# A fused matmul and rotary embedding on one core: half of the stores move to another issuing engine, two more block pairs, and GpSimd takes a slice of the multiply

## The chip, the core and the metric

The kernel runs on one core of a Trainium2 chip. That core has five engines, each with its own instruction stream: TensorE (PE in the profile), VectorE (DVE), ScalarE (ACT), GpSimd (POOL) and SyncE (SP). They wait for one another by semaphores that the kernel sets itself. DMAs are issued by SP and ACT here, each with a queue of its own (SP's is q1 in the profile, ACT's is q10: the bytes of their issues add up to the bytes of these queues); 16 DMA engines serve both queues.

The metric is the time of one execution on the device in microseconds (us). Three runs of the kernel before gave 150.59, 151.72 and 154.15 us, a median of 151.72 us. The execution that the profiler recorded took 151.62 us; its span, from the first to the last instruction, is 149.8 us.

## The reference

`x` is (16, 512, 768), the weight is 768 x 768, and there are 12 heads of 64 columns. The output is x times the weight, followed by a rotation inside each head:

```python
y = np.matmul(x, weight).reshape(batch, seq, n_heads, head_dim)
y1, y2 = y[..., :32], y[..., 32:]
out1 = y1 * cos1 - y2 * sin1
out2 = y2 * cos2 + y1 * sin2
out = np.concatenate([out1, out2], axis=-1)      # float32
```

`cos` and `sin` depend on the position in the sequence and on the column in the head, not on the batch or the head.

## The kernel before

**Tiles and groups.** The 8192 rows of x are 64 tiles of 128 rows, and four tiles are one group, so there are 16 groups (0 to 15; `LAST` is 15). The four tiles of a group have the same sequence positions and so the same cosines and sines. A group's product has 128 x 3072 values and fills six PSUM banks, ps0 to ps5, once; the next group fills the same banks again. The other two banks (pt0, pt1) hold transposed inputs.

**Two ways to transpose.** The matmul needs x with its hidden dimension on the partitions. A *single* tile is loaded whole by SP (`xs`, a ring of 11 buffers), cast to fp16 by ACT (`xc`), transposed by six PE instructions into PSUM (L232) and copied out by ACT (`xt`). A *block pair* is two tiles at once: it is loaded in four quarters of 192 KB (`xb`, a ring of 4 buffers, L201), whose rows in DRAM are cut into runs of 768 bytes, cast by ACT in one instruction (`xd`, 2 buffers) and transposed by VectorE in 32 x 32 blocks (`xp`, L252), with no work for PE. The set `BLOCKS` (L135) says which pairs (group, half) are block pairs: the second half of groups 3 to 14, and the first half of groups 5, 7, 9, 11 and 13, which makes 17 pairs. Of a block pair's quarters SP issues the first two and ACT the other two.

**Rotation.** A group's product is taken in three units of 1024 columns, u0, u1 and u2 (`units`, L259), which are banks ps0-1, ps2-3 and ps4-5. For each, VectorE multiplies the unit in PSUM by the cosines and by the sines in one instruction with 2048 results (L309), into a `tq` buffer (a ring of 5: three of their own and two in the memory of the raw weights, which the profile calls w_raw). GpSimd adds the two halves, one of them with its 32-column halves swapped, into the output buffer `ov` (L320). There are 4 `ov` buffers, one per group, so group g waits for the stores of group g - 4. Groups 14 and 15 go by smaller units, and the last three additions are VectorE's.

**Order.** One Python loop (L510) writes all instruction streams. Iteration i emits the matmuls of tile i; the rotation of a unit when its last column is done (u0 in the second tile of a group, u1 in the third, u2 in the fourth); the block transposes of pairs up to 6 tiles ahead (`bturns`); the PE transposes up to 3 tiles ahead (`turns`); and the casts up to 7 tiles ahead (`casts`). After each cast `pump` lets SP issue the loads that now have a free buffer, in the order of a sorted list; ACT's quarters come out of `casts` too. At the end of the iteration stands the group's store, if there is one: half a group (768 KB) at a time, two groups after its own, in `STORES`. Up to group 12 ACT issues all stores, later ones SP. Each engine works through its stream in order: what ACT has to wait for or is held up by delays everything that stands behind it on ACT.

The helper `Flow.do` (L42) records who wrote and read each buffer and puts the semaphore waits in front of an instruction.

Of the kernel before, what the change touches and what calls it, by code (L numbers as in the profile page):

```python
# [10 lines left out]
FP32 = mybir.dt.float32  # L11
FP16 = mybir.dt.float16
MULT = mybir.AluOpType.mult
ADD = mybir.AluOpType.add


class Flow:
# [24 lines left out]
    def do(self, e, make, reads=(), writes=(), dma=None, tick=True):  # L42
        need = {}
        for k in reads:
            for s, v in self.wrote.get(k, {}).items():
                need[s] = max(need.get(s, 0), v)
        for k in writes:
            for d in (self.wrote, self.readby):
                for s, v in d.get(k, {}).items():
                    need[s] = max(need.get(s, 0), v)  # L50
        if e == "pe":
            need.pop("pe", None)
        waits = self.settle(e, need)
        for s, v in waits[:-1]:
            self.eng[e].wait_ge(self.sem(s), v)  # L55
        i = make(self.eng[e])
        if waits:
            s, v = waits[-1]
            i.wait_op(self.sem(s), v, "sem-ge")
        name, step = (dma, 16) if dma else (e, 1)  # L60
        self.sem(name)
        at = self.count[name] + step
        if tick or dma:
            i.then_inc(self.sems[name], step)
            self.count[name] = at
            self.known[name, at] = dict(self.seen[e])
        for k in reads:
            d = self.readby.setdefault(k, {})
            d[name] = max(d.get(name, 0), at)
        for k in writes:  # L70
            self.wrote[k] = {name: at}
            self.readby[k] = {}
        return i
# [30 lines left out]
def kernel(  # L104
# [11 lines left out]
    f = Flow(nc, tc)  # L116
    do = f.do
    P = nc.NUM_PARTITIONS

    B, S, H = x.shape  # L120
    NH = int(n_heads)
    D = H // NH
# [9 lines left out]
    LAST = NG - 1  # L132


    BLOCKS = {(g, 1) for g in range(3, 15)} | {(g, 0) for g in (5, 7, 9, 11, 13)}  # L135

    def sbuf(name, shape, dt):
        return nc.alloc_sbuf_tensor(name, shape, dt).ap()

    NX, NB, NC, NCP, NXT, NXP, NTQ, NOV = 11, 4, 5, 2, 8, 4, 3, 4  # L140

    ident = sbuf("ident", [P, P], FP16)
    cold = sbuf("cold", [P, 512], FP16)
    sin_sb = sbuf("sin_sb", [P, SB, D], FP32)
    csn = sbuf("csn", [P, 2, SB, D], FP32)
# [8 lines left out]
    tq_b = [sbuf(f"tq{i}", [P, 2, 1024], FP32) for i in range(NTQ)]  # L154
    w_flat = w_raw.rearrange("p t e n -> p (t e n)")
    tq_b += [w_flat[:, ts(i, 2048)].rearrange("p (j n) -> p j n", j=2) for i in range(2)]
    W_HOME = [f"wr{t}{h}" for t, h in CHUNKS]
    ov_b = [sbuf(f"ov{i}", [P, QB * H], FP32) for i in range(NOV)]
    py = nc.alloc_psum_tensor("py", [P, 6 * 512], FP32).ap()
# [2 lines left out]
    def ring(name, n, state={}):  # L162
        k = state.get((id(f), name), 0)
        state[id(f), name] = k + 1
        return k % n

    def copy(e, o, i_):
        return lambda eng: (
            eng.copy(out=o, in_=i_) if e == "act" else eng.tensor_copy(out=o, in_=i_)  # L169
        )  # L170

    def where(i):
        g, s = divmod(i, QB)
        return QB * (g // SB) + s, g % SB

    def pair_of(i):
        return i // QB, (i % QB) // 2

    def is_block(i):
        return pair_of(i) in BLOCKS  # L180

# [55 lines left out]
    def cast_pair(gh, e="act"):  # L237
        k = xs[gh]
        c = ring("xd", NCP)
        xc[gh] = c  # L240
        do(e, copy(e, xd_b[c].rearrange("p (t j e) -> p t j e", t=NT, e=2),
                   xb_b[k].rearrange("p (j t e) -> p t j e", t=NT, e=2)),
           reads=[f"xb{k}q{q}" for q in range(NQ)], writes=[f"xd{c}"])
# [50 lines left out]

    ov_of = {}

    late = []

    def rope(g, u):
        c0, c1, ps, banks, adder = u  # L300
        w, r = c1 - c0, g % SB
        nh = w // D
        if adder == "dve":
            k = len(late)
            tq, keys = xs_b[k][:, 0 : 2 * w].rearrange("p (j n) -> p j n", j=2), [f"xs{k}"]
        else:
            k = ring("tq", NTQ + 2)
            tq, keys = tq_b[k][:, :, 0:w], [f"tq{k}"] + (W_HOME if k >= NTQ else [])
        do("dve", lambda eng: eng.tensor_tensor(  # L309
            out=tq.rearrange("p j (h d) -> p j h d", d=D),  # L310
            in0=ps.rearrange("p (h d) -> p h d", d=D)
            .unsqueeze(1).broadcast_to((P, 2, nh, D)),
            in1=csn[:, :, r, :].unsqueeze(2).broadcast_to((P, 2, nh, D)),
            op=MULT), reads=banks + ["csn"], writes=keys)
        if g not in ov_of:
            ov_of[g] = ring("ov", NOV)
        o = ov_of[g]

        def add():
            do(adder, lambda eng: eng.tensor_tensor(  # L320
                out=ov_b[o][:, ds(c0, w)].rearrange("p (h t d) -> p h t d", t=2, d=HD),
                in0=tq[:, 0].rearrange("p (h t d) -> p h t d", t=2, d=HD),
                in1=tq[:, 1].rearrange("p (h t d) -> p h t d", t=2, d=HD)[:, :, ::-1, :],
                op=ADD), reads=keys[:1], writes=[f"ov{o}c{c}" for c in range(c0, c1, 64)])

        if adder == "dve":
            late.append(add)
        else:
            add()

    def store(g, c0, c1, e):

        o = ov_of[g]
        b, r = where(g * QB)
        s0, s1 = c0 // H, -(-c1 // H)
        dst = out.rearrange("b (p r) h -> r p b h", r=SB)[r, :, b + s0 : b + s1]
        src = ov_b[o].rearrange("p (b h) -> p b h", b=QB)[:, s0:s1]
        if (c1 - c0) % H:
            dst = dst[:, 0, c0 - s0 * H : c1 - s0 * H]
            src = src[:, 0, c0 - s0 * H : c1 - s0 * H]  # L340
        do(e, lambda eng: eng.dma_start(out=dst, in_=src),
           reads=[f"ov{o}c{c}" for c in range(c0, c1, 64)], dma=f"ov{o}_{c0}")
# [5 lines left out]
        out=ident, in_=ident, compare_op=mybir.AluOpType.not_equal, fill=1.0,  # L348
# [3 lines left out]
    for k in order:  # L352
# [5 lines left out]
        out=csn[:, 0], in_=cos.rearrange("(p r) d -> p r d", r=SB)), writes=["cos"], dma="cos")  # L358
    do("sp", lambda eng: eng.dma_start(
        out=sin_sb, in_=sin.rearrange("(p r) d -> p r d", r=SB)), writes=["sin"], dma="sin")  # L360


    want = [(i, i) for i in range(QB, NTILE) if not is_block(i)]
    for g, h in BLOCKS:
        want += [(g * QB + 2 * h - 2.5 + 3 * q, ((g, h), q)) for q in (0, 1)]
# [41 lines left out]
    def castx(i, e):  # L407
        cast(i, e)
        xs_used[0] += 1
# [22 lines left out]
    for c in CHUNKS[3:5]:  # L432
# [5 lines left out]
        out=csn[:, 1, :, 0:HD], in_=sin_sb[:, :, HD:D]), reads=["sin"], writes=["csn1"])  # L438
    do("dve", lambda eng: eng.tensor_scalar_mul(
        out=csn[:, 1, :, HD:D], in0=sin_sb[:, :, 0:HD], scalar1=-1.0),  # L440
        reads=["sin", "csn1", "cos"], writes=["csn"])
    pump()

    state = {"cast": 4, "turn": 4, "bturn": 0, "half": 0}
    pairs = sorted(BLOCKS)

    def casts(upto):
        while state["cast"] < min(upto, NTILE):
            i = state["cast"]
            state["cast"] += 1  # L450
            if not is_block(i):
                castx(i, "act")
            elif i % 2 == 0:
                cast_pair(pair_of(i))
                xb_used[0] += 1
            pump()
            if state["half"] < 2 * len(pairs):
                n, q = divmod(state["half"], 2)
                g, h = pairs[n]
                if n < xb_used[0] + NB and i >= g * QB + 2 * h - LEAD:  # L460
                    load_quarter(pairs[n], 2 + q, "act")
                    state["half"] += 1
# [47 lines left out]
    for i in range(QB, NTILE):  # L510
        g, s = divmod(i, QB)
        us = units(g)
        done_to = (s + 1) * H
        for p in pieces(g, s):
            a, z, _, bank = p
            for c in CHUNKS:
                mm_piece(i, p, c, c == CHUNKS[0], c == CHUNKS[-1],
                         tick=c == CHUNKS[-1])
            for u in us:
                if u[1] == z:  # L520
                    rope(g, u)
        bturns(i + (B_AHEAD if i >= SETTLED else 3))
        turns(i + 1 + (T_AHEAD if i > QB + 1 else 2))
        casts(i + 1 + (C_AHEAD if i >= SETTLED else 3 if i == QB else 4))
        if i in STORES:
            o, k = STORES[i]
            store(o, 2 * H * k, 2 * H * (k + 1), "sp" if o > LAST - 3 else "act")
        if g == LAST:
            if s == 2:
                store(g, 0, H, "sp")  # L530
            if s == 3:
                store(g, H, 2 * H, "act")
# [3 lines left out]
    for k, add in enumerate(late):  # L536
        c = 3 * H + 256 * k
# [38 lines left out]
```

## Time and profile before

| | |
|---|---|
| median of three runs | 151.72 us |
| profiled execution, its span | 151.62 us, 149.8 us |
| busy share PE, DVE, POOL, ACT | 94%, 86%, 75%, 50% |
| mean DMA rate over the span | 355 GB/s |
| DMA rate in 45 to 110 us | 385 to 395 GB/s |
| granted TensorE clock | 0.99 |

An engine's busy share is an average over stages with different limits. What bounds a stretch is read from the chain of waits (which instruction followed which without a gap) and from the gaps in front of single instructions. A DMA's time to landing counts from its issue to its last completion signal.

### The profile page before, as it was taken

To read this page: it belongs to the slowest core of one execution; us is meant where nothing else is said; L and a number is where in the kernel's file an instruction comes from. 1 tells how busy PE (TensorE), PEld (TensorE's weight loads), DVE (VectorE), ACT (ScalarE), POOL (GpSimd) and SP (SyncE) were. 2 spreads that over 40 slices of the span, in tenths; PEclk is the share of its full clock that TensorE was granted. 3 is DMA by queue.
4 is the path that set the end of the run, shared out by engine and by line. 5 is a ranking of instruction groups with operands and counts; after the bars stand their busy time and mean duration, and the time that the engine had idled before them with its cause. 6 is when DMAs were issued, how large, how long until landed. Compare 5 with 4: busy or idle time off the path is not lost.

```text
span 149.8 us, 2471 instructions
## 1 busy us (share of the span) xinstructions
PE 141.2 (94%) x972; PEld 87.7 (59%) x972; DVE 128.7 (86%) x88; ACT 74.9 (50%) x76; POOL 112.8 (75%) x60
## 2 busy tenths in 40 slices
PE   6969999999999999999999999999999999999950
PEld 2435666666676655555666667565565666676730
DVE  0154999677999999999989999899989999998890
ACT  3444768886963280843563545444696118342100
POOL 1000299966897789887989889878988698999970
PEclk9999999999999999999999999999999999999995
DMA  4999999999999999999999999999999999997574
GB/s 129 346 400 399 404 348 293 287 297 260 227 323 399 390 373 384 388 386 387 389 382 396 391 395 396 398 385 395 399 410 410 418 413 417 396 403 311 229 278 152
DMA packets 33147, 53.11 MB, mean 355 GB/s; under 512 B 2288, under 2 KB 20464, under 8 KB 33136
## 3 DMA queue, kind: packets, MB, share of 16 engines
q10 hardware_dynamic: 16752, 27.79, 50.5%
q1 hardware_dynamic: 16384, 25.17, 48.7%
q8 instruction: 7, 0.11, 0.3%
q14 instruction: 4, 0.03, 0.1%
HBM read 27.79 MB, written 25.17 MB: 353 GB/s over the span
## 4 chain that ended last, share of the span: by engine, by line
PE 86%; DMA 5%; DVE 3%; SPq 1%; ACT 1%; issue 1%; ACTq 0%; DVEq 0%
PE py L291 80%; PE pt L232 6%; DMA w_raw<-in_weight_dram 5%; DVE xs L309 1%; ACT xc L169 1%; SPq L189 1%; DVE ov L320 1%; SPq L208 1%; DVE w_raw L309 0%; DVE w_sb L169 0%; ACTq L201 0%; DVE tq L309 0%; ACT xt L169 0%; DVEq L55 0%; SPq L571 0%
## 5 line engine op out<-in xcount | busy, mean ns | idle before, releaser
L320 POOL TENSOR_TENSOR ov<-tq 128x1024 f32<-128x1024 f32 (+2 forms) x33 | 69.0, 2107 | 27.4 <-DVE tq L309 25.7
L291 PE MATMUL py<-w_sb,xp 128*128 128x512 f16 (+1 forms) x408 | 69.4, 326 | 0.0
L309 DVE TENSOR_TENSOR tq<-py,csn 128x2048 f32<-128x2048 f32 (+2 forms) x33 | 65.8, 2015 | 3.8 <-PE py L291 3.5
L291 PE MATMUL py<-w_sb,xt 128*128 128x256 f16 (+1 forms) x360 | 60.8, 323 | 1.4 <-DVE w_sb L169 1.3
L291 PEld LDWEIGHTS py<-w_sb,xp 128*128 128x128 f16 x408 | 39.3, 98 | 24.6
L291 PEld LDWEIGHTS py<-w_sb,xt 128*128 128x128 f16 x360 | 34.2, 98 | 22.8 <-DVE w_sb L169 2.8
L320 POOL TENSOR_TENSOR ov<-w_raw 128x1024 f32<-128x1024 f32 (+2 forms) x21 | 43.6, 2087 | 4.2 <-DVE w_raw L309 4.2
L309 DVE TENSOR_TENSOR w_raw<-py,csn 128x2048 f32<-128x2048 f32 (+2 forms) x21 | 41.9, 1997 | 2.4 <-PE py L291 1.9
L169 ACT COPY xt<-pt 128x768 f16<-128x768 f16 x28 | 22.3, 800 | 31.9 <-PE pt L232 21.7
L169 ACT CAST xc<-xs 128x768 f16<-128x768 f32 x30 | 26.2, 905 | 17.7 <-issue 10.2
L169 ACT CAST xd<-xb 128x1536 f16<-128x1536 f32 x17 | 27.6, 1625 | 13.8 <-issue 5.0
L252 DVE STREAM_TRANSPOSE xp<-xd 128x768 f32<-128x768 f32 x17 | 16.4, 964 | 0.9 <-ACT xd L169 0.9
L232 PE MATMUL pt<-ident,xc 128*128 128x128 f16 x180 | 15.3, 222 | 0.2 <-ACT xc L169 0.2
L232 PEld LDWEIGHTS pt<-ident,xc 128*128 128x128 f16 x180 | 12.5, 99 | 5.2 <-ACT xc L169 1.8
L394 PE MATMUL py<-cold 128*128 128x512 f16 x12 | 5.3, 614 | 1.4 <-DVE cold L345 1.4
L169 DVE CAST w_sb<-w_raw 128x768 f16<-128x768 f32 x6 | 3.4, 558 | 3.5 <-DMA w_raw<-in_weight_dram 3.5
L169 DVE COPY xt<-pt 128x768 f16<-128x768 f16 x2 | 1.1, 558 | 5.6 <-PE pt L232 5.6
L394 PEld LDWEIGHTS py<-cold 128*128 128x128 f16 x12 | 1.6, 144 | 3.6 <-issue 2.2
L169 ACT ACT_TABLE_LOAD x1 | 1.3, 1283 | 0.9 <-SPq L114 0.9
L291 PE MATMUL pt<-w_sb,xt 128*128 128x256 f16 x12 | 1.5, 272 | 0.0
L309 DVE TENSOR_TENSOR xs<-pt,csn 128x512 f32<-128x512 f32 x2 | 1.3, 680 | 0.0
L291 PEld LDWEIGHTS pt<-w_sb,xt 128*128 128x128 f16 x12 | 1.2, 98 | 0.1
(11 smaller groups left out, 3.4 us busy)
## 6 DMA issues: line engine op xcount, KB each, us to landing
out_dram<-ov ACTq DMA_DIRECT2D x26, 768.0 KB, 13.7
xs<-in_x_dram SPq DMA_DIRECT2D x30, 384.0 KB, 9.8
xb<-in_x_dram SPq DMA_DIRECT2D x34, 192.0 KB, 8.2
xb<-in_x_dram ACTq DMA_DIRECT2D x34, 192.0 KB, 10.2
out_dram<-ov SPq DMA_DIRECT2D x4, 768.0 KB, 5.1
w_raw<-in_weight_dram SPq DMA_DIRECT2D x6, 384.0 KB, 7.5
out_dram<-ov SPq DMA_DIRECT2D x1, 384.0 KB, 2.3
out_dram<-ov ACTq DMA_DIRECT2D x1, 384.0 KB, 2.3
```

The lines of the kernel that those rows point to most:

```text
L169: eng.copy(out=o, in_=i_) if e == "act" else eng.tensor_copy(out=o, in_=i_)
L189: do(e, lambda eng: eng.dma_start(out=xs_b[k], in_=x[b].rearrange("(p r) h -> r p h", r=SB)[r]), writes=[f"xs{k}"], dma=f"xs{k}")
L208: do(e, lambda eng: eng.dma_start(out=w_raw[:, t, h], in_=wv[t, h]), writes=[f"wr{t}{h}"], dma=f"w{t}{h}")
L232: do("pe", lambda eng: eng.transpose(pt[:, t, h, :], src[:, t, h, :], ident), reads=[f"xc{c}", "ident"], writes=[f"pt{k}"], tick=(t, h) == ...
L252: do("dve", lambda eng: eng.transpose(out=dst, in_=src), reads=rd, writes=[f"xp{z}"])
L291: do("pe", lambda eng: eng.matmul(ps, get(t, h), w_sb[:, t, h, a - s * H : z - s * H], start=start, stop=stop), reads=[key, f"w{t}{h}"], w ...
L309: do("dve", lambda eng: eng.tensor_tensor(out=tq.rearrange("p j (h d) -> p j h d", d=D), in0=ps.rearrange("p (h d) -> p h d", d=D) .unsque ...
L320: do(adder, lambda eng: eng.tensor_tensor(out=ov_b[o][:, ds(c0, w)].rearrange("p (h t d) -> p h t d", t=2, d=HD), in0=tq[:, 0].rearrange(" ...
L394: do("pe", lambda eng: eng.matmul(py[:, ts(b, 512)], cold[:, 0:P], cold, start=True, stop=warmed[0] < WARM - 6), reads=["cold"], writes=[f ...
```

## The change

It has three parts.

First, the second half of each of the groups 0 to 12 (columns 1536 to 3071) is stored by a DMA that SP issues in place of ACT. The place in the loop stays. The first halves stay with ACT.

Second, `BLOCKS` gets two more pairs, the first halves of groups 6 and 10. Tiles 24, 25, 40 and 41 are no longer single tiles, and in groups 5 to 7 and 9 to 11 all tiles are in block pairs.

Third, in groups 2 to 9 VectorE multiplies only the first 896 columns of u2. ACT copies the last 128 columns from bank ps5 to a new buffer `yb` (two of them), GpSimd multiplies them there into the same `tq` buffer, and then does the addition of the whole unit. These three instructions are held back and emitted after the casts of the iteration, ahead of its store. The copy on ACT also waits for VectorE's part of the multiply.

```diff
-    BLOCKS = {(g, 1) for g in range(3, 15)} | {(g, 0) for g in (5, 7, 9, 11, 13)}
+    BLOCKS = {(g, 1) for g in range(3, 15)} | {(g, 0) for g in (5, 6, 7, 9, 10, 11, 13)}
...
+    PART = 128
...
+    yb_b = [sbuf(f"yb{i}", [P, PART], FP32) for i in range(2)]
...
-        do("dve", lambda eng: eng.tensor_tensor(
-            out=tq.rearrange("p j (h d) -> p j h d", d=D),
-            in0=ps.rearrange("p (h d) -> p h d", d=D)
-            .unsqueeze(1).broadcast_to((P, 2, nh, D)),
-            in1=csn[:, :, r, :].unsqueeze(2).broadcast_to((P, 2, nh, D)),
-            op=MULT), reads=banks + ["csn"], writes=keys)
+        def times(e, y, a, z, rd, wr):
+            n = (z - a) // D
+            do(e, lambda eng: eng.tensor_tensor(
+                out=tq[:, :, a:z].rearrange("p j (h d) -> p j h d", d=D),
+                in0=y.rearrange("p (h d) -> p h d", d=D)
+                .unsqueeze(1).broadcast_to((P, 2, n, D)),
+                in1=csn[:, :, r, :].unsqueeze(2).broadcast_to((P, 2, n, D)),
+                op=MULT), reads=rd + ["csn"], writes=wr)
+
+        part = c0 == 2048 and 2 <= g <= 9
+        m = w - PART if part else w
+        times("dve", ps[:, 0:m], 0, m, banks, keys)
...
+        def rest():
+            do("act", copy("act", yb_b[y], ps[:, m:w]), reads=banks[-1:] + keys[:1], writes=[f"yb{y}"])
+            times("pool", yb_b[y], m, w, [f"yb{y}"], [keys[0] + "p"])
+            add()
+
+        if part:
+            keys = [keys[0], keys[0] + "p"]
...
-                op=ADD), reads=keys[:1], writes=[f"ov{o}c{c}" for c in range(c0, c1, 64)])
+                op=ADD), reads=keys[: 2 if part else 1], writes=[f"ov{o}c{c}" for c in range(c0, c1, 64)])
+        if part:
+            held.append(rest)
+        elif adder == "dve":
...
+        while held:
+            held.pop()()
         if i in STORES:
             o, k = STORES[i]
-            store(o, 2 * H * k, 2 * H * (k + 1), "sp" if o > LAST - 3 else "act")
+            store(o, 2 * H * k, 2 * H * (k + 1), "sp" if k or o > LAST - 3 else "act")
```

More of the change, by code (lines that the diff above doesn't have):

```diff
@@ L295 @@
     ov_of = {}
-    late = []
+    late, held = [], []
     def rope(g, u):
@@ L317, in rope @@
         o = ov_of[g]
+        if part:
+            y = ring("yb", 2)
+        def rest():
[4 more added lines that the diff above has]
+            keys = [keys[0], keys[0] + "p"]
         def add():
@@ L323, in add @@
                 in1=tq[:, 1].rearrange("p (h t d) -> p h t d", t=2, d=HD)[:, :, ::-1, :],
-                op=ADD), reads=keys[:1], writes=[f"ov{o}c{c}" for c in range(c0, c1, 64)])
-        if adder == "dve":
+                op=ADD), reads=keys[: 2 if part else 1], writes=[f"ov{o}c{c}" for c in range(c0, c1, 64)])
+        if part:
+            held.append(rest)
+        elif adder == "dve":
             late.append(add)
```

## The prediction

> **What bounds the kernel now.** I read the chain that ended last first, because PE's busy share alone (94%) doesn't say whether PE waits. In order of time, from 57 us:
>
> ```profile
> 57.98 1.95 PE py L291 x12
> 59.93 0.34 PE pt L232 x6
> 60.27 13.65 PE py L291 x84
> 73.92 0.34 PE pt L232 x6
> 74.25 1.95 PE py L291 x12
> 76.20 0.34 PE pt L232 x6
> ```
>
> Columns: start, length, what. The chain stays on PE without a gap: a tile's twelve matmuls take 1.95 us, a single tile's transposes 0.34 us, and nobody else appears from 25.9 to 142.3 us. PE sets the time, and two groups (eight tiles, two of them single) take 8 x 1.95 + 2 x 0.34 = 16.28 us.
>
> Second, the busy times by stage, in stretches of two groups, show who is close behind:
>
> ```profile
> 61.30:77.55 16.25, 16.25 (x110) 10.06 (x108) 16.07 (x10) 8.45 (x8) 14.15 (x7) 1.00 1.06 388
> 77.55:93.85 16.30, 16.30 (x110) 10.08 (x109) 15.89 (x10) 8.05 (x8) 14.20 (x7) 1.00 1.06 394
> ```
>
> After the length come PE, weight loads, VectorE, ACT, GpSimd, granted clock, DMA share and GB/s. VectorE works 16.0 of 16.3 us, GpSimd 14.2, and the DMA engines are never free (share over 1, as packets overlap) at about 390 GB/s. Eight loaded tiles and eight stored ones are 16 x 384 KB = 6.29 MB, which in 16.28 us is 386 GB/s: DMA has one or two per cent to spare.
>
> Third, GpSimd's timeline near the end:
>
> ```profile
> 117.58 4.70 POOL L320 TENSOR_TENSOR ov<-tq 128x1024 f32<-128x1024 f32 x2 [1.71 <-DMA out_dram<-ov]
> 122.24 4.70 POOL L320 TENSOR_TENSOR ov<-w_raw 128x1024 f32<-128x1024 f32 x2
> 127.37 4.77 POOL L320 TENSOR_TENSOR ov<-tq 128x1024 f32<-128x1024 f32 x2 [0.43 <-DVE tq L309]
> ```
>
> Group 12's u0 waited 1.71 us for the store of group 8 to leave its buffer. From 127.37 us GpSimd works without a gap to 145.28 us. So from the second addition of group 12 on GpSimd has 0.43 us to spare, and what delays it more pushes its end.
>
> **Part 1: two more block pairs.** Four single tiles lose their PE transposes: 4 x 0.34 = **1.36 us off the path that sets the end**, at about 57.7, 59.9, 90.2 and 92.5 us. ACT loses 4 casts (905 ns) and 4 copies (800 ns) and gains 2 pair casts (1625 ns): 3.57 us less, off the path. VectorE gains 2 transposes, 2 x 0.96 = 1.93 us.
>
> Can VectorE take that? Start to start its multiply takes 2.20 us and its transpose 0.89. From group 3's u2 to group 5's u2 it must do six multiplies (two of them shorter, below) and four transposes: 6 x 2.20 - 2 x 0.26 + 4 x 0.89 = 16.24 us, while PE now takes 16.28 - 0.68 = 15.6. VectorE ends up 0.65 us late, and in the next two groups, with three transposes against 16.28 us of PE, it regains 0.9. PE comes back to a bank 5.2 us after it filled it (four sixths of a group of 7.8), the multiply takes 2.2, so 3 us late would still be hidden. I cost this at 0; without the cover it is 0.65 us.
>
> The DMA side costs more. A pair's 768-byte runs move slower: 20 to 36 us, mostly quarters, ran at 295 GB/s, 10 to 20 us, mostly whole tiles, at 402. For 786 KB that is 2.67 against 1.96 us, so two pairs cost 1.4 us of DMA time, while PE wants its data 1.36 us sooner. With one or two per cent spare this lands on what is queued last.
>
> **Part 2: GpSimd's 128 columns.** VectorE's 2048-, 1024- and 512-result rows (2270, 1221, 680 ns) give 1.03 ns a result: 256 fewer save 0.26 us, eight times 2.1 us, which pays for the two transposes. GpSimd's new multiply has 256 results; no such multiply is in the trace. The nearest of the groups by form is the 256-wide addition (count, busy time, mean ns):
>
> ```profile
> L320 POOL TENSOR_TENSOR ov<-tq 128x256 f32<-128x256 f32 x2 | 1.4, 716 | 0.0
> ```
>
> The 512-wide one, 1270 ns, is the upper bound; the lower is half of this row, if one broadcast input costs nothing. I take 0.72, eight times 5.7 us. A group costs GpSimd 3 x 2.35 + 0.72 = 7.77 us against 7.8 to 8.5 of PE: just enough.
>
> ACT's new copy of 128 columns: the casts of 768 and 1536 columns (905, 1625 ns) make 0.94 ns a column and 185 ns fixed, about 0.3 us (a sixth of the 800 ns copy is the lower bound, that copy the upper). Its *wait* matters more: it stands behind a pair cast and a quarter's issue, waits for VectorE, and bank ps5 is refilled only after it. Queued behind it on ACT are the next casts, copies and first-half stores. Let T be when PE ends group g. PE needs ps5 again 1.3 us (two thirds of a tile) before the next group ends, at T + 6.5. VectorE is done at about T + 2.6. ACT's pair cast in this iteration began at T + 1.4 to T + 3.4 (group 5: 65.57 against 62.2). With 1.63 of cast, 0.4 of issue and 0.3 of copy the bank is free at T + 3.7 to 5.8. It fits, by 0.7 us at worst. So 0.
>
> GpSimd's u2 thus starts as late as T + 5.8 rather than T + 2.3. The lag can be no larger than that, five tq buffers allow about 9 us, and from group 10 on it shrinks by 0.75 us a group or more. By group 12 it is 116 us against the 115 when VectorE delivers: nearly gone.
>
> **Part 3: the stores on SP.** ACT loses 13 issues, 10.2 MB; with its quarters of the two pairs it keeps 18.4 of 27.8 MB, SP goes from 25.2 to 34.6. ACT gains time (its store issues took 845 ns median, up to 3.5 us, as its queue was full; the free value is 0.34), but all off the path, since PE didn't wait for ACT. SP gains 13 issues of 0.4 us; its own waits add to over 55 us for free `xb` buffers, and a store stands behind them no longer than ACT's place in the order. The data is ready: group o's u2 is added by T + 9, SP reaches the store at T + 12 or later. What is queued behind the store on SP is loads, and they now share their queue with 768 KB pieces. How the queues share, in 0.6 us around 79 us:
>
> ```profile
> q10 hardware_dynamic: 72, 0.18, 76.8%
> q1 hardware_dynamic: 72, 0.05, 26.5%
> ```
>
> Packets, MB, share: one packet each in turn, so a queue with 768-byte pieces (SP's q1) gets a fifth or a quarter of the bytes beside stores. The rule in the Trainium skill, DMA: Bandwidth & Descriptors, section Issuing engines are not separate DMA queues, says that transfers of all issuers interleave on the same 16 engines and that a second issuer saves only issue time. It speaks against this part, and by it alone the sum would be the second rival's; the two rows agree with the interleaving, but show that the bytes follow the packet size.
>
> Where it counts is group 8's second half. On ACT it was issued at 102.6 and landed at 119.4. On SP it stands behind six whole tiles, the last of which landed at 119.0. DMA time is lost to part 1, so I take 119.4 + 1.4 = 120.8 us. Lower bound: 119.4; upper: another store, at the 1.9 us between landings of stores there, slips ahead, 122.7.
>
> **The sum.** Group 12's u1 starts at 120.8; three additions of 2.35 later, at 127.85, group 13's u1, which was at 127.37. GpSimd's end moves to 145.76; its last store takes 1.8, and 1.6 us lie between the last landing and the end: a span of 149.2. VectorE's path ends at 149.8 - 1.36 = 148.4. So the span is 149.2, 0.6 less, and the execution **151.62 - 0.6 = 151.0 us**. With the bounds: 150.3 (119.4; PE's gain in full) to 152.9 (122.7). The profiled execution is 0.1 below the median of three, 151.72; about 2%, 3 us, is what a measurement of this kernel tells from no change.
>
> **Rivals.**
> 1. *Quarters come late* (slower). In the groups that are all block pairs a pair's buffer is freed eight tiles before its own cast, where it was ten. The last quarter in a row on SP takes 12.3 to 12.7 us to land (that of 63.0, that of 95.3). For pair (11, 1) its buffer is free at 83.5, the issue at 84.4, the landing at 97.0, cast, issue and copy are done at 99.3; PE, now 1.36 us early, needs ps5 at 99.9. That is 0.6 us of slack (2.2 in group 6). If a store stands ahead on SP, at half rate 3.8 us, PE stalls 3.2 there and 1.6 in the first stretch: 4.8 us, 150.3 + 4.8 = **155.1 us** (GpSimd's wait for the store is hidden behind these stalls). Decisive point: a landing over 13.2 us. For: DMA never idles, and ACT waited 1.3 us for a quarter even before. Against: ACT's lighter queue takes fewer turns, and ACT is freer to cast early.
> 2. *The queue is irrelevant* and nothing is late: the rows' PE gain alone, **150.3 us**. For: DMA conserves work, and loads ran about 10 us ahead at the end. Against: the 1.71 us wait.
> 3. *GpSimd is later*, by a dearer multiply or the store's upper bound: **152.9 us**.
>
> More than 1.36 us can't be won: PE had no other gaps.
>
> **How the numbers follow.** Forecast 0.42, rival 1 0.25 (spread 153 to 159), rival 2 0.18, rival 3 0.15. Forecast, rivals 2 and 3 lie within 2%, of rival 1 most above it: faster by over 2% 0.03, within 0.75, slower 0.22. The range from 149.6 (rival 2 with the runs' own scatter) to 156.0 leaves out about a sixth.
>
> **What would show it.** PE's transposes fall from 180 to 156 (26 tiles). PE's chain without gaps: rival 1 is wrong; idle PE or stretched matmuls ended by ACT's copy or cast in 60 to 70 and 90 to 102 us: right. GpSimd's wait for `out_dram` near 118 us and its start of group 13's u1 show the store's term; the 128-column multiply's row its price; landings of SP's quarters over 13 us would make the forecast wrong.

## The result, and the profile after

The changed kernel takes **157.73 us** (median of four executions, 157.52 to 159.48) against 152.47 us for the kernel before (four, 150.59 to 154.15: the three on record and one more): a ratio of **1.046, 95% interval 1.0345 to 1.0574**. The forecast was 151.0 us in a range of 149.6 to 156.0, with 0.22 for slower by over 2%. The forecast and the range are both wrong. All ratios here leave out the longer executions of both kernels, so that of e5, whose ten executions scatter from 151.01 to 155.27 us, lies below the ratio of its medians; the profiled executions of e5 and e9 are among those left out.

The profiled execution took 159.48 us, its span 157.7 us, which is 7.9 more than before. By the medians the change costs 157.73 - 152.47 = 5.3 us. The page of the changed kernel, engines first (busy us, share, instructions), then the chain by engine:

```profile
PE 140.1 (89%) x948; PEld 85.8 (54%) x948; DVE 130.8 (83%) x90; ACT 74.0 (47%) x78; POOL 117.9 (75%) x68
...
DMA 49%; DVE 12%; POOL 9%; ACT 9%; issue 8%; PE 4%; SPq 4%; ACTq 2%; DVEq 0%; POOLq 0%
```

PE fell from 94% to 89%, though it has 24 transposes fewer (156 for 180), and the chain, which was PE for most of the span, is now half DMA. The stages tell more (start and end, length, PE, PEld, VectorE, ACT, GpSimd, clock, DMA share, GB/s), the first two for the stretches shown of before:

```profile
61.30:77.55 16.25, 16.25 (x109) 10.07 (x108) 16.06 (x10) 7.25 (x9) 16.09 (x9) 1.00 1.06 371
77.55:93.85 16.30, 16.30 (x101) 9.67 (x99) 16.18 (x11) 7.76 (x7) 15.10 (x9) 1.00 1.06 390
93.85:110.10 16.25, 15.60 (x106) 9.57 (x105) 14.70 (x9) 7.78 (x8) 14.71 (x8) 1.00 1.07 353
110.10:127.00 16.90, 16.90 (x112) 10.35 (x111) 16.77 (x11) 9.88 (x10) 10.85 (x5) 1.00 1.04 389
```

PE is busy in all of them but for 0.65 us in the third. Up to 127 us PE has lost next to nothing against before: it ended group 13 at 127.61 us, before at 127.30. The engine that stands out is GpSimd in the last row, 10.85 of 16.90 us. Its timeline there (start, length, what, idle time before and what released it):

```profile
115.50 2.37 POOL L340 TENSOR_TENSOR ov<-w_raw 128x1024 f32<-128x1024 f32 x1 [1.58 <-DVE xp L255]
...
128.44 2.36 POOL L340 TENSOR_TENSOR ov<-tq 128x1024 f32<-128x1024 f32 x1 [5.91 <-DVE tq L315]
130.76 4.69 POOL L340 TENSOR_TENSOR ov<-w_raw 128x1024 f32<-128x1024 f32 x2
```

The addition at 128.44 is group 12's u1, which before began at 119.91. From it GpSimd works without a gap to 153.19 us (before 145.28): **7.9 us later, all of the longer span**. The 5.91 us are put down to VectorE, but its product had been there since some 121 us. What landed just before 128.44 is group 8's second half. Its issue and its time to landing, after and before (length of the issue in ns, start; then us to landing):

```profile
L363 SPq DMA_DIRECT2D out_dram<-ov x1: 492/492/492, 113.5 to 113.5; - x1
...
DMA to landing us min/median/max: 14.9/14.9/14.9
```

```profile
L341 ACTq DMA_DIRECT2D out_dram<-ov x1: 1997/1997/1997, 102.6 to 102.6; - x1
...
DMA to landing us min/median/max: 16.7/16.7/16.7
```

So it was issued by SP at 113.49 and landed at 128.37; before, ACT issued it at 102.63 and it landed at 119.36. Group 12 writes into group 8's `ov` buffer, and u1 is the first unit that touches the second half. The trace names the last releaser that it can match; here it was the other one, the store. The 1.58 us above is the same wait one group earlier (group 7's second half landed at 115.44).

Why the store was late is seen in SP's own timeline, after and then before (start, length of the issue, what):

```profile
103.02 0.47 SPq L204 DMA_DIRECT2D xb<-in_x_dram  x1
103.53 2.17 SPq L192 DMA_DIRECT2D xs<-in_x_dram  x2
106.11 0.33 SPq L204 DMA_DIRECT2D xb<-in_x_dram  x1
106.48 6.97 SPq L192 DMA_DIRECT2D xs<-in_x_dram  x4
113.49 7.11 SPq L363 DMA_DIRECT2D out_dram<-ov  x4
```

```profile
99.83 0.97 SPq L189 DMA_DIRECT2D xs<-in_x_dram  x2
100.85 0.44 SPq L201 DMA_DIRECT2D xb<-in_x_dram  x1
101.33 2.00 SPq L189 DMA_DIRECT2D xs<-in_x_dram  x4
```

The six whole tiles (the last whole tiles of the program, with one quarter among them) were issued back to back in about 0.47 us each; now they take up to 2.1 us each. I read it as SP waiting for room in its queue. The store is issued behind them at 113.49 rather than at 102.63 by ACT, and then still needs 14.9 us to land. From 60 to 100 us the two queues (packets, MB, share of 16 engines) moved this, after and before:

```profile
q1 hardware_dynamic: 5933, 8.10, 58.9%
q10 hardware_dynamic: 5717, 6.53, 47.4%
```

```profile
q10 hardware_dynamic: 6797, 11.01, 73.0%
q1 hardware_dynamic: 4712, 4.57, 32.4%
```

SP's queue (q1) was the light one, 4.57 MB, and has become the heavy one, 8.10 MB. All queues together moved less, 14.67 MB in place of 15.62. That lower rate is not what costs the time: of the runs below, e3 (14.73 MB) and e9 (14.72) moved as little in these 40 us and lost nothing, while e2 (15.47) lost 3.6%.

### The profile page after: what moved, and what is told of

Its sections match the earlier page's. It is cut to its first block, busy times and chain, and to the rows that moved or that the text cites. A ratio compares the mean times of both kernels' runs of the same rounds, so it can differ in the third digit from the quotient of the medians.

```text
span 157.7 us, 2441 instructions
## 1 busy us (share of the span) xinstructions
PE 140.1 (89%) x948; PEld 85.8 (54%) x948; DVE 130.8 (83%) x90; ACT 74.0 (47%) x78; POOL 117.9 (75%) x68
## 4 chain that ended last, share of the span: by engine, by line
DMA 49%; DVE 12%; POOL 9%; ACT 9%; issue 8%; PE 4%; SPq 4%; ACTq 2%; DVEq 0%; POOLq 0%
DMA xb<-in_x_dram 44%; POOL ov L340 9%; ACT xd L172 7%; DMA w_raw<-in_weight_dram 5%; PE py L294 4%; DVE w_raw L315 4%; DVE tq L315 4%; DVE xp L255 2%; DVE ov L340 2%; SPq L192 2%; ACTq L204 2%; SPq L204 1%; DVE xs L315 1%; ACT xt L172 1%; ACT xc L172 1%
## 5 line engine op out<-in xcount | busy, mean ns | idle before, releaser
L294 PE MATMUL py<-w_sb,xp 128*128 128x256 f16 (+1 forms) x456 | 76.4, 326 | 0.6 <-ACT yb L172 0.6
L315 DVE TENSOR_TENSOR tq<-py,csn 128x2048 f32<-128x2048 f32 (+3 forms) x33 | 64.8, 1982 | 5.7 <-POOL ov L340 3.2
L294 PEld LDWEIGHTS py<-w_sb,xp 128*128 128x128 f16 x456 | 44.1, 98 | 29.1 <-ACT yb L172 0.9
L294 PE MATMUL py<-w_sb,xt 128*128 128x256 f16 (+1 forms) x312 | 52.9, 322 | 4.2 <-DVE w_raw L315 2.6
L315 DVE TENSOR_TENSOR w_raw<-py,csn 128x2048 f32<-128x2048 f32 (+3 forms) x21 | 40.9, 1947 | 3.9 <-PE py L294 1.6
L172 ACT CAST xd<-xb 128x1536 f16<-128x1536 f32 x19 | 31.0, 1629 | 25.7 <-DMA xb<-in_x_dram 17.2
L294 PEld LDWEIGHTS py<-w_sb,xt 128*128 128x128 f16 x312 | 29.3, 98 | 23.0 <-DVE w_raw L315 2.8
L172 ACT CAST xc<-xs 128x768 f16<-128x768 f32 x26 | 22.9, 901 | 22.0 <-DMA xs<-in_x_dram 13.7
L172 ACT COPY xt<-pt 128x768 f16<-128x768 f16 x24 | 19.1, 801 | 13.5 <-PE pt L235 10.3
L340 DVE TENSOR_TENSOR ov<-xs 128x256 f32<-128x256 f32 x3 | 3.0, 1055 | 0.0
```

The lines of the kernel that those rows point to most:

```text
L294: do("pe", lambda eng: eng.matmul(ps, get(t, h), w_sb[:, t, h, a - s * H : z - s * H], start=start, stop=stop), reads=[key, f"w{t}{h}"], w ...
L315: do(e, lambda eng: eng.tensor_tensor(out=tq[:, :, a:z].rearrange("p j (h d) -> p j h d", d=D), in0=y.rearrange("p (h d) -> p h d", d=D) . ...
L340: do(adder, lambda eng: eng.tensor_tensor(out=ov_b[o][:, ds(c0, w)].rearrange("p (h t d) -> p h t d", t=2, d=HD), in0=tq[:, 0].rearrange(" ...
```

## The experiments

Two theories. **A, the store:** the time is lost because group 8's second half lands late behind SP's loads and holds back GpSimd; in its narrow form that one store is enough. **B, rival 1:** part 1's late quarters and part 3's ACT and PE stalls cost the time along the whole way. In all runs the table's columns come from the profiled execution: landing of group 8's second half, start of group 12's u1, GpSimd's end, the span; then the median and the ratio to the kernel before on the same chip.

| run | landing | u1 of 12 | GpSimd's end | span | median | ratio [95%] |
|---|---|---|---|---|---|---|
| before | 119.36 | 119.91 | 145.28 | 149.8 | 152.47 | |
| after | 128.37 | 128.44 | 153.19 | 157.7 | 157.73 | 1.046 [1.0345, 1.0574] |
| e1 parts 1 and 2 | 120.02 | 120.75 | 145.59 | 150.1 | 151.02 | 0.9915 [0.9878, 0.9953] |
| e2 part 3 | 125.01 | 125.08 | 149.84 | 154.4 | 157.23 | 1.0362 [1.0311, 1.0412] |
| e3 late stores on ACT | 118.32 | 120.13 | 145.09 | 150.5 | 151.27 | 0.991 [0.986, 0.996] |
| e4 two stores on SP | 123.54 | 123.60 | 148.73 | 153.1 | 155.64 | 1.0235 [1.0186, 1.0283] |
| e5 four loads behind | 121.97 | 122.04 | 149.12 | 153.5 | 153.64 | 0.9971 [0.9921, 1.0022] |
| e6 part 1 | 118.36 | 119.38 | 144.88 | 149.4 | 151.39 | 0.9965 [0.9938, 0.9992] |
| e7 part 2 | 118.70 | 119.48 | 145.06 | 149.6 | 151.81 | 0.999 [0.9951, 1.0029] |
| e8 copy first | 119.52 | 120.06 | 144.9 | 149.4 | 151.61 | 0.9972 [0.9941, 1.0003] |
| e9 one store back | 115.37 | 121.41 | 147.05 | 151.4 | 151.88 | 0.999 [0.9949, 1.0032] |
| e10 e3 and copy first | 117.98 | 118.75 | 144.35 | 150.1 | 151.48 | 0.9941 [0.9894, 0.9988] |
| e11 e3 without the slice | 115.81 | 119.45 | 144.96 | 149.5 | 151.47 | 0.9981 [0.9942, 1.002] |

From the start of u1 to GpSimd's end it is 24.75 to 25.64 us in every row but e5's (27.08): when u1 starts late, the end is late by as much. GpSimd's end and the span go together: in before, after and nine of the eleven runs the span ends 4.3 to 4.6 us after it (e3 5.4 and e10 5.8, where the last additions are no later and what stands behind them is).

**e1, the change without part 3.**

```diff
-            store(o, 2 * H * k, 2 * H * (k + 1), "sp" if k or o > LAST - 3 else "act")
+            store(o, 2 * H * k, 2 * H * (k + 1), "sp" if o > LAST - 3 else "act")
```

> The changed kernel with all stores of groups 0 to 12 issued by ACT again; the two pairs and GpSimd's slice stay. Theory A (the second half of group 8 stands behind loads in SP's queue, its late landing holds up GpSimd's addition of group 12's u1, and from there GpSimd's work sets the end): the store is issued near 103 us and lands by 121, u1 of group 12 starts by 121 instead of 128.4, and the time is 150 to 152 us. Theory B (the two extra pairs make the quarters late, ACT, VectorE and PE stall, and the stores are a side show): it stays near the changed kernel, 155 to 158 us.

151.02 us, 0.9915 of before. GpSimd from 116 us on:

```profile
116.10 7.02 POOL L340 TENSOR_TENSOR ov<-tq 128x1024 f32<-128x1024 f32 x3
123.08 4.71 POOL L340 TENSOR_TENSOR ov<-w_raw 128x1024 f32<-128x1024 f32 x2
127.76 5.91 POOL L340 TENSOR_TENSOR ov<-tq 128x1024 f32<-128x1024 f32 x3
```

No wait is left there. Parts 1 and 2 alone give what was forecast for all three, so the pairs, B's first half, cost nothing by themselves.

**e2, part 3 alone.** The kernel before, with the changed line of the stores.

```diff
-            store(o, 2 * H * k, 2 * H * (k + 1), "sp" if o > LAST - 3 else "act")
+            store(o, 2 * H * k, 2 * H * (k + 1), "sp" if k or o > LAST - 3 else "act")
```

> The kernel before with the second-half stores of groups 0 to 12 on SP, and nothing else changed. Theory A: SP's queue is as loaded as in the changed kernel, group 8's second half lands after 126 us, and the time is 155 to 158 us. Theory B: without the extra pairs nothing is late, 150 to 153 us.

157.23 us. GpSimd's two waits are there, and here the trace names the store:

```profile
112.17 2.37 POOL L320 TENSOR_TENSOR ov<-w_raw 128x1024 f32<-128x1024 f32 x1 [2.38 <-DMA out_dram<-ov]
...
125.08 2.37 POOL L320 TENSOR_TENSOR ov<-tq 128x1024 f32<-128x1024 f32 x1 [5.86 <-DMA out_dram<-ov]
```

Moving 13 issues from ACT to SP costs 3.6% (3.1 to 4.1) by itself, with no other edit.

**e3, the stores of groups 7 to 12 back on ACT.**

```diff
-            store(o, 2 * H * k, 2 * H * (k + 1), "sp" if k or o > LAST - 3 else "act")
+            store(o, 2 * H * k, 2 * H * (k + 1), "sp" if (k and o < 7) or o > LAST - 3 else "act")
```

> The changed kernel with only the second halves of groups 0 to 6 on SP; those of groups 7 to 12 go back to ACT. Theory A: only the stores of groups 7 and 8 are needed soon enough to hurt, so nearly all comes back, 150 to 152.5 us. If the whole of SP's load counts (loads late since group 3), it keeps half or more of the loss, 154 to 157 us.

151.27 us, as e1. Seven stores on SP up to group 6 cost nothing that can be measured; the loss is in the later six.

**e4, only groups 7 and 8 on SP.**

```diff
-            store(o, 2 * H * k, 2 * H * (k + 1), "sp" if k or o > LAST - 3 else "act")
+            store(o, 2 * H * k, 2 * H * (k + 1), "sp" if (k and o in (7, 8)) or o > LAST - 3 else "act")
```

> The changed kernel with only the second halves of groups 7 and 8 on SP, the other eleven back on ACT. Theory A in its narrow form: these two alone stand behind the last loads, group 8's lands after 125 us and the time is 155 us or more. If SP's queue must have been filled by the earlier stores before its loads are held up: near 151 to 153 us.

155.64 us. The store's issue, start and time to landing:

```profile
L363 SPq DMA_DIRECT2D out_dram<-ov x1: 1334/1334/1334, 102.3 to 102.3; - x1
...
DMA to landing us min/median/max: 21.3/21.3/21.3
```

```profile
123.60 2.37 POOL L340 TENSOR_TENSOR ov<-tq 128x1024 f32<-128x1024 f32 x1 [6.29 <-DMA out_dram<-ov]
```

The most telling run: the store is issued at 102.27, as early as by ACT before (102.63), and SP's queue isn't held up by eleven other stores. Still it lands 4.2 us later than before, and 3.5 later than in e1, which differs only in who issues the second halves of groups 7 and 8. The six whole tiles ahead of it are hardly late here (the last was issued at 101.79, took 18.0 us and landed at 119.83 us, before at 118.95), and the store comes 3.7 us behind them. So of the 9.0 us by which the landing moved in the change, 3.5 to 4.2 are due to the place behind the tiles, without any late issue; the other 4.8 come with the eleven other stores on SP, which delay the tiles themselves (the last landed at 125.19 in the change). The time is as expected; the landing was expected after 125 us and came earlier.

**e5, four loads behind the store.** All stores as in the change, but the whole tiles 60 to 63 may be issued only after group 8's second half.

```diff
+    at_tile = [0]
...
-                if xs_sent[0] - xs_used[0] >= NX:
+                if xs_sent[0] - xs_used[0] >= NX or j >= 60 and at_tile[0] <= 42:
...
+        at_tile[0] = i
```

> The changed kernel, all second halves still on SP, but the loads of the last four tiles (60 to 63) are emitted on SP behind group 8's second-half store instead of ahead of it; they are needed from 126 us on. Theory A: what the store stands behind is the cause. Four whole tiles less ahead of it are 1.6 MB, 4 us at 400 GB/s or up to 8 at half of that: it is issued near 106 us, lands at 121 to 124, and the time falls from 157.6 to 151 to 154 us. If the store is late for SP's total load rather than for these loads, the time stays at 156 to 158.

The landing moves from 128.37 to 121.97:

```profile
122.04 2.38 POOL L340 TENSOR_TENSOR ov<-tq 128x1024 f32<-128x1024 f32 x1 [0.91 <-DMA out_dram<-ov]
...
130.96 5.92 POOL L340 TENSOR_TENSOR ov<-tq 128x1024 f32<-128x1024 f32 x3 [1.87 <-DMA out_dram<-ov]
```

The same store by the same engine in the same kernel, with four loads fewer ahead of it, is 6.4 us earlier. The next one (group 9's second half, now behind those loads) then costs 1.87 us in the profiled execution, which took 155.27 us. By the median the order recovers 157.73 - 153.64 = 4.1 us, by the ratio of 0.997 all of the loss; how much of it is left isn't settled, that most of it hangs on the order within SP's queue is.

**e6 and e7, part 1 alone and part 2 alone**, each put into the kernel before: e6 has the first of these lines alone, e7 the second with what belongs to it (the slice, the copy, the held addition).

```diff
+    BLOCKS = {(g, 1) for g in range(3, 15)} | {(g, 0) for g in (5, 6, 7, 9, 10, 11, 13)}
...
+        part = c0 == 2048 and 2 <= g <= 9
```

> The kernel before with the two extra block pairs alone, stores on ACT, no slice for GpSimd. By the recorded sum PE saves 1.36 us and VectorE, without the shorter multiplies, has 1.93 us more to do but hides it: 0.5 to 1.4 us faster than before, ratio 0.991 to 0.997. If VectorE becomes the bound without the slice, ratio 1.00 to 1.01.

> The kernel before with GpSimd's slice of the multiply alone (groups 2 to 9), stores on ACT, 17 block pairs. PE sets the time and loses no work, so nothing is gained: ratio 0.997 to 1.003. If the wait for ACT's copy holds up PE here too, as the trace with all stores on ACT shows for 1.0 us near 100 us, ratio 1.003 to 1.01.

0.9965 and 0.999: neither costs anything, part 1 gains at most 0.6% by its interval, part 2 alone gains nothing that can be told. Together (e1) they have 0.85%.

**e8, ACT's copy ahead of its casts.** In e1 PE has one gap, and ACT's timeline says why:

```profile
101.26 2.12 PE L294 MATMUL py<-w_sb,xp 128*128 128x512 f16 x9 [1.02 <-ACT yb L172]
```

```profile
98.90 1.60 ACT L172 CAST xd<-xb 128x1536 f16<-128x1536 f32 x1 [3.50 <-issue]
...
100.94 0.27 ACT L172 COPY yb<-py 128x128 f32<-128x128 f32 x1 [0.44 <-ACT xd L172]
```

PE waits for bank ps5, which the `yb` copy frees, and the copy stands behind a pair's cast and ACT's issues. That is rival 1's mechanism. e8 emits the copy first, on top of e1:

```diff
+        while held:
+            held.pop()()
         casts(i + 1 + (C_AHEAD if i >= SETTLED else 3 if i == QB else 4))
-        while held:
-            held.pop()()
```

> The changed kernel with all stores on ACT and the held copy, multiply and addition emitted ahead of the iteration's casts rather than behind them. If the 1.0 us for which PE waited near 100 us comes from ACT's copy standing behind a pair cast and DMA issues, PE has no gap there and the time is 0.5 to 1.2 us below that of the kernel with the stores on ACT (151.0): 149.8 to 150.5 us, ratio 0.983 to 0.988. If something else holds PE's bank, it stays at 151.

A miss. PE's gap at 100 us is gone, but the ratio is 0.9972, no better than e1's 0.9915. GpSimd waits 2.11 us for group 8's *first* half:

```profile
117.74 4.71 POOL L340 TENSOR_TENSOR ov<-tq 128x1024 f32<-128x1024 f32 x2 [2.11 <-DMA out_dram<-ov]
```

PE ends group 13 at 126.15 us, 1.3 earlier than in e1 (127.47), and the ratio shows none of it. I read this as PE's gap being covered by GpSimd, whose own wait for a store takes its place; the intervals of e1 and e8 overlap, so the two runs don't prove it.

**e9, one store back on ACT.** All of the change, but group 8's second half.

```diff
-            store(o, 2 * H * k, 2 * H * (k + 1), "sp" if k or o > LAST - 3 else "act")
+            store(o, 2 * H * k, 2 * H * (k + 1), "sp" if (k and o != 8) or o > LAST - 3 else "act")
```

> The changed kernel with one store moved: group 8's second half is issued by ACT again, the other twelve second halves stay on SP. Theory A: group 12's u1 no longer waits for it (start near 120 instead of 128.4 us). If that one store is all, the time is 150.5 to 152 us. If SP's later stores are late in the same way, group 9's second half (landed at 130.9 us) holds up group 13's u1 next, which then starts near 131 instead of 135.4 us: 153 to 155 us.

151.88 us, 0.999. Twelve stores stay on SP and the loss is gone: one 768 KB store is worth 157.73 - 151.88 = 5.85 us by the medians, with the other twelve in the queue. Its landing is at 115.37, earlier than before; group 12's u1 doesn't wait any more, and group 13's waits 0.42 us for the next store:

```profile
128.88 5.93 POOL L340 TENSOR_TENSOR ov<-tq 128x1024 f32<-128x1024 f32 x3 [0.42 <-DMA out_dram<-ov]
```

That is theory A in its narrow form. It also speaks against B: the last whole tile lands at 125.66, as late as in the change, and ACT waits 13.6 us in eight waits for SP's quarters (15.2 in eight in the change), and yet nothing is lost.

**e10 and e11, can more be had?** e10 is e3 with e8's order (both edits below); e11 is e3 without part 2 (the first edit below alone, on a kernel without the slice).

```diff
+            store(o, 2 * H * k, 2 * H * (k + 1), "sp" if (k and o < 7) or o > LAST - 3 else "act")
...
+        while held:
+            held.pop()()
         casts(i + 1 + (C_AHEAD if i >= SETTLED else 3 if i == QB else 4))
```

> All three parts, with second halves on SP for groups 0 to 6 only, and the held copy, multiply and addition emitted ahead of the casts. If PE's wait for ACT's copy still costs time, 0.5 to 1 us below the kernel with only the first seven second halves on SP (151.3): ratio 0.983 to 0.988. If GpSimd's end sets the time and not PE, the same ratio as that kernel, 0.990 to 0.998.

> The two extra pairs and second halves on SP for groups 0 to 6, without GpSimd's slice. If the slice is worth something beside the pairs, this is slower than the kernel with it (ratio 0.991): 0.995 to 1.000. If the slice only delays GpSimd, this is the fastest of all: 0.983 to 0.990.

0.9941 and 0.9981. Neither beats e3 or e1, whose 0.991 and 0.9915 are the lowest of all; all these gains are under 1%. Whether part 2 helps when it is added to part 1 stays open: e3 against e11 has it so by the ratios, but their intervals overlap.

## Why the prediction was wrong

**The step that failed** is the landing of group 8's second half, "119.4 + 1.4 = 120.8", upper bound 122.7. It landed at 128.37. The prediction said rightly that the store stands behind six whole tiles, and that GpSimd has 0.43 us to spare from there on; but it took the landing of the six tiles (119.0) from the trace of before, as if the stores put into SP's queue earlier changed nothing for the loads behind them. It did say that the loads "now share their queue with 768 KB pieces", but gave that no price. The cost was there: SP's bytes between 60 and 100 us rose from 4.57 to 8.10 MB, the last of the six loads was issued at 112.5 in place of 102.8 and landed at 125.2, 6.2 us later, and the store 3.2 us behind it. That second distance, 3.7 us in e4, the sum had as 120.8 - 119.0 = 1.8 (upper bound 3.7); the first, 6.2 us, it had as nothing. The 1.4 us of DMA time put down to the pairs isn't seen: the landing is 118.36 with the pairs alone (e6).

**"SP gains 13 issues of 0.4 us"** was mis-sized for the same reason: a store's issue on SP has a median of 0.45 us, but of those ahead of the store that counts one took 2.60 (at 63.47), and a quarter's between 35 and 106 us took up to 2.49 (before 0.52).

**"VectorE's path ends at 149.8 - 1.36 = 148.4"**, beside GpSimd's, was wrong too. The last three additions are VectorE's, have two inputs in SBUF and are slowed while GpSimd is adding. Their line after and before (minimum, median, maximum ns; first and last start):

```profile
L340 DVE TENSOR_TENSOR ov<-xs x3: 410/411/2344, 151.1 to 153.7; 128x256 f32<-128x256 f32 x3
```

```profile
L320 DVE TENSOR_TENSOR ov<-xs x3: 415/419/420, 145.2 to 145.8; 128x256 f32<-128x256 f32 x3
```

Before, GpSimd is done at 145.28 and each takes 0.42 us. After, the first begins at 151.12 and ends at 153.46, GpSimd's last addition at 153.19. So VectorE's end hangs on GpSimd's, and the sum "145.76, its last store takes 1.8, and 1.6" lacked some 0.95 us of VectorE's additions behind GpSimd; made with the rows of before it would have given 145.28 + 1.8 + 1.6 = 148.7 for a span of 149.8, and so have shown the gap. The Trainium skill, SBUF — State Buffer, section Who interferes with whom, says that GpSimd's only SBUF port pair is VectorE's second one, held exclusively; the 0.42 against 2.34 us agree.

**The rule that spoke against this change** was given too much. The Trainium skill, DMA: Bandwidth & Descriptors, section Issuing engines are not separate DMA queues, says that DMAs of all issuers interleave on the same engines and that a second issuer saves only the issue time. The prediction let it stand as its rival 2, "the queue is irrelevant", with 0.18. e2 speaks against that here: which issuer a store is on is worth 3.6%. The interleaving may hold all the same; what the rule leaves out is that whole tiles and stores of one issuer landed in the order of their issue, in all thirteen traces.

**What held.** Part 1: PE's transposes fell by 24. In e4, where PE has no gap, it ran from group 3's end to group 13's in 80.01 us against 81.35 before, 1.34 of the 1.36 us. In the changed kernel it took 81.25 us and in e1 81.39, so nearly all of that gain was lost again; stalls of 0.25 and 0.65 us (1.02 in e1) are most of it. The times of e6 and e1, 151.39 and 151.02 us, are near the forecast's 151.0, but that e1 hits it is partly luck, since the sum lacked the 0.95 us above. Part 2's prices were right, 0.72 us forecast for the multiply, 0.3 for the copy:

```profile
L315 POOL TENSOR_TENSOR w_raw<-yb,csn 128x256 f32<-128x256 f32 x4 | 2.9, 727 | 5.0 <-ACT yb L172 5.0
...
L172 ACT COPY yb<-py 128x128 f32<-128x128 f32 x8 | 2.1, 266 | 3.4 <-ACT xd L172 2.6
```

VectorE's shorter multiply takes 2.01 to 2.02 us, 0.26 less than 2.27, as forecast.

**Rivals.** Rival 1 named the right place and the right stall (ACT's copy late, ps5, PE), but its size is 0.65 us after and 1.02 in e1, not 4.8, and e8, where that stall is gone, is no faster. So the copy's wait, "It fits, by 0.7 us at worst. So 0.", was a term set too low, though not the one that made the loss. (ACT did wait for SP's quarters, 15.2 us in eight waits between 35 and 106 us against 1.3 in one, and PE stalled for little of it.) Rival 3 named the right mechanism, "the store's upper bound", with a bound too low by 5.7 us. The warning sign that the prediction wrote down itself, GpSimd's wait for `out_dram` near 118 us, came true, though at u1 (from 122.5 to 128.4 us) and not at u0. The other one came too: between 35 and 106 us SP's quarters took up to 15.5 us to land, over the 13 that it named (before up to 14.0); but e9, where they take up to 17.2, loses nothing by it.

**What stays open:** no run tells what holds up SP's issues. And e1's profiled execution (151.89 us, span 150.1) lies 0.9 us above its median, so no trace itemises its gain of 0.85%; that GpSimd's end sets it is shown only in the sense that every run's span follows that end.

## What to carry to other kernels

Here the whole tiles and stores of each issuer landed in the order of their issue. So a transfer that is moved to another issuer stands behind the bytes ahead of it there, and it delays what is issued behind it; neither side's issue and landing times may be taken over from the old trace. Find for each moved store who waits for its buffer to be free, and move only those with slack (here seven early ones were free and a single late one, on top of the others, cost 5.85 us). When a wait in a trace is put down to an engine that had finished long before, look for the DMA that landed in the same tenth of a microsecond.

## What the runs showed of the hardware

- An issue isn't a fixed price: on SP the issue of one of the last six whole tiles took 0.43 to 0.51 us where SP's queue had moved 4.57 MB from 60 to 100 us, and up to 2.1 us where it had moved 8.10. That a full queue holds up the issuing engine is how I read it; no run sets the queue's depth.
- A store that was issued at 102.27 us by SP took 21.3 us to land (e4), one issued by ACT at 102.63 took 16.7 us (before; 16.5 in e1, at 103.52). It is the same store, but for the queue that it stood in and what was ahead of it there. In all thirteen traces the whole tiles and stores of one issuer landed in the order of their issue; the quarters' landings can't be told apart by issuer.
- One VectorE addition of 256 columns with both inputs in SBUF took 0.41 us alone and 2.34 us beside GpSimd's last additions, of which three ran meanwhile; it ended 0.27 us after the last. In e4 the two engines seem to take turns: VectorE's three additions needed 0.94 to 0.98 us each, two of GpSimd's three 0.90 and 0.91 in place of 0.73.
